# Four in place of six seven-product pairs in the fourth group of the convolution's input

## The chip, the cores and the metric

The kernel runs on one core of a Trainium2 chip. The metric is device time in microseconds (us) from start to end of one execution; the time of a kernel is the median of its runs. Engines are named as the profile names them: PE (TensorE, matmuls), PEld (its weight loads), DVE (VectorE), ACT (ScalarE), POOL (GpSimd), SP (the queue that issues the loads).

## The reference, cut to what matters

One layer with two halves side by side, 256 rows of 4096 columns. Seven column blocks of one large weight `w_in` are multiplied with the normalised input; the convolution half needs the blocks `a_c` and `g_c`.

```python
xn = rms_norm(h, norm_in_g[i])
proj = xn @ w_in[i]                       # 256x4096 @ 4096x14336
q, k, v, z_a, a_c, g_c, z_c = jnp.split(proj, ...)
y_a = rms_norm(chunked_attention(q, k, v, rel_table[i]), attn_out_g[i]) * silu(z_a)
y_c = rms_norm(conv_module(a_c, g_c, ...), conv_out_g[i]) * silu(z_c)
h = h + concatenate([y_a, y_c]) @ w_out[i]
h = h + sigmoid(rms_norm(h) @ w_ple_gate[i] + b) * (p[i] @ w_ple[i])
# conv_module: u = a * sigmoid(g); causal depthwise convolution of 31 taps;
# layer norm; silu; u @ w_pw + b_pw
```

## The kernel before

All large products have 256 rows and 4096 (or 2048) rows of weights. `mixed_product` makes one such product for two column blocks of 512 at once (a *group*). It walks the 4096 weight rows as sixteen *pairs* of 128-row blocks in the order of a list such as `early`. Every float32 operand is split in a high and a low part (`wh`, `wl` of weights, `uh`, `ul` of sums of weights), and each product is three matmuls of 128x128 by 128x512: high by high, low by high, high by low (line 372).

- A pair without a star is *plain*: 2 row halves x 2 column blocks x 2 weight blocks = 8 products, 24 matmuls. Its two weight tiles are each split by one ACT cast and one DVE subtraction of 128x1024 (lines 204 and 205).
- A starred pair (*seven*) is done by a scheme of Strassen's kind with 7 products, 21 matmuls. For that, DVE forms four sums of weights (`ua`, `ub`, lines 428, 429, 432, 433), ACT and DVE split the two sum tiles (again lines 204 and 205), and four combinations of the pair's x are needed.
- The combinations of x for one pair are six DVE instructions (line 280, then 257 to 260, and 266) and one ACT cast (265). For pairs 0, 2, 4 and 6 they are made in the first group and kept for all later ones.

The groups run in this order: convolution input 1 (`glu_conv(0)`, ends near 103 us of the span), 2 (to 191 us), queries and keys, values, attention 0, convolution input 3, convolution input 4 (454 to 546 us), queries and keys 1, attention 1, and so on to attention 3 near 930 us, where the pointwise convolution (`w_pw`) starts. At the end of each convolution group DVE finishes the four results `z` (496), multiplies by the gate (707), PE transposes (714) and ACT copies to `uT` (719).

The convolution itself is elementwise DVE work, 124 instructions for each group (the *taps*, lines 678 and 682). Taps and other small jobs wait in the list `later`; `fill(n)` takes n of them at the end of each pair, by `early_fills` (64 in all for a group). Behind the taps stand the jobs of the layer norm: sums, mean, variance (775), spread (788), `swish` (DVE 793, ACT 794) and `split` (ACT 804, DVE 805). The program is written in that order, and a scheduler of the framework then sets the order on each engine; every engine works its own list strictly in that order.

In `glu_conv(3)` (the fourth group) the list is `early_six`: pairs 8 and 10 have stars too, and `more_combinations` makes the x combinations for them inside the group, ahead of pairs 7 and 9, as four jobs at the head of `later`.

Of the kernel before, what the change touches and what calls it, by code (L numbers as in the profile page):

```python
# [11 lines left out]
F32R = mybir.dt.float32r  # L12
# [4 lines left out]
P = 128  # L17
NB = 512
# [7 lines left out]
def hybrid_block(  # L26
# [24 lines left out]
    _, T, D = x.shape  # L51
    NH = T // P
    AW = attn_out_g.shape[1]
    CW = conv_out_g.shape[1]
# [13 lines left out]
    def pool(name, bufs, stack=ctx, side=0, **kw):  # L68
        return stack.enter_context(tc.tile_pool(name=name, bufs=bufs, side=sides[side], **kw))

    cpool = pool("cpool", 1)
    act = pool("act", 8)
# [13 lines left out]
    def tmp_psum():  # L86
        return ps_tmp.tile([P, 512], F32, tag="tmp", name="tmp_ps")
# [7 lines left out]
    o_a, o_g, o_zc = 4 * AW, 4 * AW + CW, 4 * AW + 2 * CW  # L95
    w_in0 = w_in[0]
# [83 lines left out]
    later = deque()  # L180
# [95 lines left out]
    def combine_again(dst, at, t, i, rows, then=lambda ins: None):  # L276

        a, s = rows
        then(
            nc.vector.tensor_tensor(  # L280
                a.rearrange("q (i t) -> q i t", t=T), t[:, i : i + 2, 0, :].bitcast(F32),
                t[:, i : i + 2, 1, :].bitcast(F32), ALU.add,
            )
        )
        return combined_parts(dst, at, s, a[:, :T], a[:, T : T + P], a[:, T + P :], 1.0, then)
# [27 lines left out]
    def units(text):  # L313

        return [(int(u.rstrip("*")), u.endswith("*")) for u in text.split()]
# [2 lines left out]
    dense = units("1 0* 3 2* 5 4* 6* 7 8* 9 10* 11 12* 14* 13 15")  # L318
    first = units("0 1 3 5 7 9 11 13 15 2* 8 4* 10 6* 12 14")
    early = units("1 3 5 7 0* 9 2* 11 4* 13 6* 15 8 10 12 14")  # L320
    early_six = units("1 3 5 7 0* 9 2* 11 4* 13 6* 15 8* 10* 12 14")

    valued = units("1 3 5 7 8 0* 9 2* 10 4* 11 6* 12 13 14 15")

    early_fills = (4, 6, 7, 1, 5, 1, 5, 1, 5, 1, 2, 4, 6, 6, 6, 4)
# [155 lines left out]
    def scaled_pair(w, col, apart, order, r, fills, home={}, then=lambda: None, **kw):  # L481

        t, z = [], []

        def on_helpers(helper):
            for dst, src in zip((t, z), sum_tiles(**home)):
                dst.extend(src)
            then()
            nc.scalar.activation(z[0][0], helper["P1"], AF.Identity, scale=r[:, :1])
            helper_sums(helper, z)  # L490
            for h, j in QUARTERS[1:]:
                nc.scalar.activation(z[h][j], z[h][j], AF.Identity, scale=r[:, h : h + 1])

        c = mixed_product(w, col, xT, xS, order, on_helpers, fills=fills, apart=apart, **kw)
        for h, j in QUARTERS:
            stt(
                z[h][j], c[h][j], r[:, h : h + 1], z[h][j],
                ALU.mult, ALU.subtract if j else ALU.add,
            )
        return t  # L500
# [16 lines left out]
    xS = {}  # L517
# [6 lines left out]
    r_x = cpool.tile([P, NH], F32, name="r_x")  # L524

    def combinations(c, then=lambda ins: None):

        rest = []

        def begin():  # L530
            rows = spool.tile([P, 2, NB], F32, tag="stage", name="comb")
            rest.append(
                combine_again(*xS[2 * c], xT[c], 0, (rows[:, 0], rows[:, 1]), then)
            )

        return begin, lambda: rest.pop()()
# [147 lines left out]
                cv[:, i, PAD - k :], ALU.mult, ALU.add,  # L684
            )

    def more_combinations(pair):

        if pair in (7, 9):
            c = (pair + 1) // 2  # L690
            xS[2 * c] = act.tile([P, 2, 2, T], F32R, tag="act", name="comb_x"), 0
            later.extendleft(reversed(combinations(c)))

    def glu_conv(c):
        if c == 0:
            sg, gate = scaled_pair(
                w_in0, o_a, o_g - o_a, first, r_x, (1,), begin=first_pairs
            )
        else:
            last = c == CW // NB - 1  # L700
            sg, gate = scaled_pair(
                w_in0, o_a + c * NB, o_g - o_a, early_six if last else early, r_x, early_fills,
                ahead=more_combinations if last else None,
            )
        for h in range(NH):
            nc.scalar.activation(gate[:, h, :], gate[:, h, :], AF.Sigmoid)
            tt(sg[:, h, :], sg[:, h, :], gate[:, h, :], ALU.mult)
        uT = spool.tile([P, 4, T], F32, tag="hd", name="uT", bufs=5)
        for pair in range(2):
            pt = tmp_psum()  # L710
            for i in range(2):
                for h in range(NH):
                    b = 2 * pair + i
                    nc.tensor.transpose(
                        pt[:, i * T + h * P : i * T + (h + 1) * P],
                        sg[:, h, b * P : (b + 1) * P],
                        ident,
                    )
            nc.scalar.copy(
                uT[:, 2 * pair : 2 * pair + 2, :], pt.rearrange("q (i t) -> q i t", t=T)  # L720
            )
        cv = act.tile([P, 4, T], F32, tag="act", name="cv")
        for i in range(4):
            for k in reversed(range(TAPS)):
                later.append(partial(conv_tap, cv, uT, i, 4 * c + i, k))
        conv.append(cv)
# [201 lines left out]
    n_g = H // GH  # L928
    assert n_g == CW // NB == 4
    glu_conv(0)  # L930
    glu_conv(1)
    load_bias(0)
    keys(0, early_fills)
    values(0, early, early_fills, home=dict(tag="hd", bufs=5))
    attention(0)
    glu_conv(2)
    glu_conv(3)
    load_bias(1)
# [69 lines left out]
    xS = [xS[0][0]]  # L1008
# [22 lines left out]
    def before_last(make):  # L1031

        return lambda pair: make(0) if pair == dense[-1][0] else None
# [20 lines left out]
    for ys, o_z, r_y in ((y_a, o_za, r_a), (y_c, o_zc, r_c)):  # L1054
        for c0 in range(0, len(ys), 2):
            last = ys is y_c and c0 + 2 == len(ys)
# [27 lines left out]
    for c0 in range(0, D // NB, 2):  # L1084
        for j in range(2):
            hc = act.tile([P, NH, NB], F32, tag="act", name="hc")
            c = c0 + j
# [5 lines left out]
        def on_helpers(helper):  # L1093
# [10 lines left out]
            ahead=y_ahead if c0 == 0 else before_last(h_ahead) if c0 + 2 == D // NB else None,  # L1104
# [205 lines left out]
```

## Time and profile before

| | |
|---|---|
| median of 3 runs | 2048.03 us (2047.39 to 2050.57) |
| the profiled execution | 2048.88 us, its span 2047.1 us |
| PE busy | 2022.0 us (99%), 9082 matmuls recorded |
| PEld busy | 1656.1 us (81%) |
| DVE busy | 1943.8 us (95%) |
| ACT busy | 1195.2 us (58%) |
| mean granted clock of PE | 0.996 |

The busy time of PE counts overlapping matmuls once, so idle time of PE is read from gaps ahead of single matmuls, and slow stretches from the granted clock. A row of the timeline gives start, length, engine, line, what is written and read, and in square brackets how long the engine idled just before and what ended that. A row of the chain of waits gives a start, a length and the instruction that the end of the stretch was waiting for at that time.

### The profile page before, as it was taken

The page shows a single profiled execution, that of the slowest core. Times are in us where ns is not written, and L with a number is a line of the kernel's source. Part 1 is how long each engine was busy: PE and PEld are TensorE (multiplying, and loading weights), DVE is VectorE, ACT ScalarE, POOL GpSimd, SP SyncE. Part 2 cuts the span into 40 slices and gives each one's busy share as a digit, 9 for nine tenths or more (in the row PEclk, how much of TensorE's full clock was granted, in tenths as well). Part 3 has the DMA queues.
Part 4 walks back from the last instruction along what each step waited for, and adds up shares of the span by engine and source line. Part 5 has one row for each costly group of instructions (what it writes and reads, how often), then busy time and mean ns, then how long its engine had stood idle before and what let it go on. Part 6 is the DMA issues. An engine that isn't in the chain of part 4 may idle for free.

```text
span 2047.1 us, 26034 instructions
## 1 busy us (share of the span) xinstructions
PE 2022.0 (99%) x9082; PEld 1656.1 (81%) x9082; DVE 1943.8 (95%) x2784; ACT 1195.2 (58%) x1543; POOL 8.1 (0%) x19
## 2 busy tenths in 40 slices
PE   9999999999999999999999999999999999999997
PEld 7888888888778888878888888888888888888876
DVE  7999999989999999889899999999999999999998
ACT  7655545655555544676565656676565666655555
POOL 0000000000000000000000000000000000000000
PEclk9999999999999999999999999999999999999998
DMA  8666666566665666645666666676666656666765
GB/s 288 192 197 205 204 192 200 165 203 185 192 187 170 199 198 183 191 155 199 192 213 210 193 214 200 216 242 208 214 198 206 204 188 208 199 220 205 235 207 179
DMA packets 157758, 412.30 MB, mean 201 GB/s; under 512 B 12974, under 2 KB 16190, under 8 KB 157626
## 3 DMA queue, kind: packets, MB, share of 16 engines
q1 hardware_dynamic: 156976, 409.80, 63.5%
q8 instruction: 71, 1.16, 0.2%
q10 hardware_dynamic: 650, 0.84, 0.1%
q14 instruction: 61, 0.50, 0.1%
HBM read 406.39 MB, written 4.19 MB: 201 GB/s over the span
## 4 chain that ended last, share of the span: by engine, by line
PE 88%; DVE 7%; issue 2%; DMA 1%; ACT 1%; SPq 0%; POOL 0%; POOLq 0%; ACTq 0%; DVEq 0%
PE acc L372 69%; PE acc_P L372 16%; DVE wl L205 2%; DVE cv L682 2%; PE tmp_ps L170 1%; DVE ul L205 1%; PE acc L218 1%; DMA wt<-in_w_in_dram 1%; DVE ub L433 0%; PE tmp_ps L835 0%; PE tmp_ps L851 0%; DVE ub L432 0%; DMA wt<-in_w_out_dram 0%; ACT wh L204 0%; PE tmp_ps L869 0%
## 5 line engine op out<-in xcount | busy, mean ns | idle before, releaser
L372 PE MATMUL acc<-wh,big_t 128*128 128x512 f32 x4196 | 1296.9, 392 | 2.5 <-ACT wh L204 1.0
L204 ACT CAST wh<-wt 128x1024 fp32r<-128x1024 f32 (+1 forms) x737 | 711.1, 976 | 561.0 <-PE acc L372 416.2
L372 PEld LDWEIGHTS acc<-wh,big_t 128*128 128x128 f32 x4196 | 784.9, 188 | 166.3 <-ACT wh L204 1.8
L205 DVE TENSOR_TENSOR wl<-wt,wh 128x1024 fp32r<-128x1024 f32 (+1 forms) x737 | 819.5, 1123 | 36.6 <-ACT wh L204 32.4
L372 PE MATMUL acc<-wl,big_t 128*128 128x512 f32 x2098 | 805.6, 392 | 2.8 <-DVE wl L205 2.7
L372 PEld LDWEIGHTS acc<-wl,big_t 128*128 128x128 f32 x2098 | 393.4, 188 | 87.8 <-DVE wl L205 6.1
L682 DVE SCALAR_TENSOR_TENSOR cv<-uT,dw,cv 128x255 f32<-128x255 f32 (+22 forms) x480 | 212.1, 460 | 1.0
L204 ACT CAST uh<-ub 128x1024 fp32r<-128x1024 f32 x130 | 136.7, 1052 | 114.0 <-DVE ub L433 97.4
L204 ACT CAST uh<-ua 128x1024 fp32r<-128x1024 f32 x130 | 136.9, 1053 | 82.2 <-DVE ua L429 76.5
L205 DVE TENSOR_TENSOR ul<-ub,uh 128x1024 fp32r<-128x1024 f32 x130 | 158.4, 1219 | 7.0 <-ACT uh L204 6.3
L372 PE MATMUL acc_P<-uh,big_t 128*128 128x512 f32 x528 | 161.6, 393 | 0.0
L205 DVE TENSOR_TENSOR ul<-ua,uh 128x1024 fp32r<-128x1024 f32 x130 | 158.3, 1218 | 0.8 <-ACT uh L204 0.2
L372 PEld LDWEIGHTS acc_P<-uh,big_t 128*128 128x128 f32 x528 | 97.4, 188 | 24.3 <-ACT uh L204 5.1
L428 DVE TENSOR_TENSOR ua<-wt 128x512 f32<-128x512 f32 x130 | 89.0, 685 | 18.1 <-DMA wt<-in_w_in_dram 11.4
L372 PE MATMUL acc_P<-ul,big_t 128*128 128x512 f32 x264 | 101.1, 394 | 1.2 <-DVE ul L205 1.2
L429 DVE TENSOR_TENSOR ua<-wt 128x512 f32<-128x512 f32 x130 | 88.7, 683 | 1.8 <-DMA wt<-in_w_in_dram 1.1
L433 DVE TENSOR_TENSOR ub<-ub,wt 128x512 f32<-128x512 f32 x130 | 88.9, 684 | 0.9
L432 DVE TENSOR_TENSOR ub<-ua,wt 128x512 f32<-128x512 f32 x130 | 88.7, 683 | 0.3
L372 PE MATMUL acc<-uh,big_t 128*128 128x512 f32 x260 | 80.6, 390 | 0.0
L372 PE MATMUL acc_P<-wh,big_t 128*128 128x512 f32 x260 | 80.4, 389 | 0.0
L372 PE MATMUL acc_P<-uh,comb_t 128*128 128x512 f32 x228 | 69.8, 391 | 0.1
L372 PEld LDWEIGHTS acc_P<-ul,big_t 128*128 128x128 f32 x264 | 49.2, 188 | 15.2 <-DVE ul L205 5.0
(240 smaller groups left out, 1370.1 us busy)
## 6 DMA issues: line engine op xcount, KB each, us to landing
wt<-in_w_in_dram SPq DMA_DIRECT2D x447, 512.0 KB, 4.2
wt<-in_w_out_dram SPq DMA_DIRECT2D x128, 512.0 KB, 4.1
wt<-in_w_ple_gate_dram SPq DMA_DIRECT2D x128, 512.0 KB, 4.2
wt<-in_w_pw_dram SPq DMA_DIRECT2D x32, 512.0 KB, 4.5
hc<-in_x_dram SPq DMA_DIRECT2D x8, 512.0 KB, 5.8
wt<-in_w_ple_dram SPq DMA_DIRECT2D x8, 512.0 KB, 4.5
xin<-in_x_dram SPq DMA_DIRECT2D x7, 512.0 KB, 7.9
out_dram<-hc SPq DMA_DIRECT2D x12, 256.0 KB, 2.8
```

The lines of the kernel that those rows point to most:

```text
L170: nc.tensor.transpose(pt[:, i * T + h * P : i * T + (h + 1) * P], src[:, h, b] if len(src.shape) == 4 else src[:, h, b * P : (b + 1) * P], ...
L204: nc.scalar.copy(wh[:, :kc, :], wt[:, :kc, :]),
L205: nc.vector.tensor_tensor(wl[:, :kc, :], wt[:, :kc, :], wh[:, :kc, :].bitcast(F32), ALU.subtract),
L218: nc.tensor.matmul(acc, a, b[:, k, :], start=kb == 0 and kind == 0, stop=kb == kblocks - 1 and kind == 2,)
L372: nc.tensor.matmul(banks[name], a, b, start=name not in begun, stop=final and ends[name] == n and kind == 2 and not (left and name in "P2 ...
L428: plus(ua[:, 0], w0[:, 0], w0[:, 1])
L429: plus(ua[:, 1], w0[:, 1], w1[:, 1])
L432: plus(ub[:, 0], ua[:, 0], w1[:, 1])
L433: plus(ub[:, 1], ub[:, 0], w1[:, 0])
L682: nc.vector.scalar_tensor_tensor(cv[:, i, PAD - k :], uT[:, i, : T + k - PAD], dw[:, b, k : k + 1], cv[:, i, PAD - k :], ALU.mult, ALU.add,)
```

## The change

The fourth group uses the list `early`, as the second and third groups do: pairs 8 and 10 become plain. `more_combinations` and its four jobs at the head of `later` are gone, and with them the two tiles `comb_x`. Nothing else is edited. Lines behind the first removed one move up by one, and those behind `more_combinations` by nine: in the rows below 371 is the old 372, 677 and 681 are 678 and 682, 785 is 794.

```diff
     early = units("1 3 5 7 0* 9 2* 11 4* 13 6* 15 8 10 12 14")
-    early_six = units("1 3 5 7 0* 9 2* 11 4* 13 6* 15 8* 10* 12 14")
...
-    def more_combinations(pair):
-
-        if pair in (7, 9):
-            c = (pair + 1) // 2
-            xS[2 * c] = act.tile([P, 2, 2, T], F32R, tag="act", name="comb_x"), 0
-            later.extendleft(reversed(combinations(c)))
-
...
-            last = c == CW // NB - 1
             sg, gate = scaled_pair(
-                w_in0, o_a + c * NB, o_g - o_a, early_six if last else early, r_x, early_fills,
-                ahead=more_combinations if last else None,
+                w_in0, o_a + c * NB, o_g - o_a, early, r_x, early_fills,
+                
             )
```

Since each fill takes as many jobs as before, all later jobs come four places earlier, and the scheduler sets a different order from the fourth group (454 us) up to the pointwise convolution (about 1000 us). Three places matter below.

DVE at the start of the fourth group, behind the gate's products (`comb` is a combination of x, `cv` a tap). Before:

```order
L280 TENSOR_TENSOR comb<-big_t 128x512
L678 TENSOR_SCALAR cv<-uT,dw,prm 128x256
L257 TENSOR_TENSOR comb<-comb 128x128
L682 SCALAR_TENSOR_TENSOR cv<-uT,dw,cv 128x255
L258 SCALAR_TENSOR_TENSOR comb<-comb 128x128
L682 SCALAR_TENSOR_TENSOR cv<-uT,dw,cv 128x254
L205 TENSOR_TENSOR wl<-wt,wh 128x1024
```

The same place with the change:

```order
L677 TENSOR_SCALAR cv<-uT,dw,prm 128x256 x2
L681 SCALAR_TENSOR_TENSOR cv<-uT,dw,cv 128x255 x2
L681 SCALAR_TENSOR_TENSOR cv<-uT,dw,cv 128x254
L205 TENSOR_TENSOR wl<-wt,wh 128x1024
L681 SCALAR_TENSOR_TENSOR cv<-uT,dw,cv 128x253
L681 SCALAR_TENSOR_TENSOR cv<-uT,dw,cv 128x254
```

Taps have taken the places of the combinations. From the last `z` of the third group to the last `z` of the fourth, DVE's list had 147 instructions, 57 of them taps; it now has 138, 72 of them taps. That is, in kind and number, the list of the second group (138, 72 taps), and nearly in its order. PE has 375 instructions between the last transposes of the third and fourth groups before and 381 now; the second group has 386.

ACT behind the spread of the layer norm (`rs`), near 882 us, up to the second weight cast (`wh`) that follows it. Before:

```order
L743 ACTIVATE rs<-tmp_ps 128x256
L204 CAST wh<-wt 128x1024
L794 ACT_TABLE_LOAD
L794 ACTIVATE cv<-cv,prm 128x256 x3
L492 ACTIVATE z<-z,r_x 128x512
L794 ACTIVATE cv<-cv,prm 128x256 x2
L492 ACTIVATE z<-z,r_x 128x512 x2
L794 ACTIVATE cv<-cv,prm 128x256 x6
L204 CAST wh<-wt 128x1024
L794 ACTIVATE cv<-cv,prm 128x256 x4
```

With the change:

```order
L734 ACTIVATE rs<-tmp_ps 128x256
L204 CAST wh<-wt 128x1024
L785 ACT_TABLE_LOAD
L785 ACTIVATE cv<-cv,prm 128x256 x7
L491 ACTIVATE z<-z,r_x 128x512 x3
L785 ACTIVATE cv<-cv,prm 128x256 x8
L204 CAST wh<-wt 128x1024
L785 ACTIVATE cv<-cv,prm 128x256
```

Fifteen swishes in place of eleven now stand ahead of the second cast. On PE the first matmul that reads this cast is the 45th behind the spread's transposes before, and the 49th now.

PE at the first head of attention 3, near 909 us (`kT,qT` the scores, `ident,s` the transposes of the softmax, `acc_80..` the first pair of the pointwise convolution). Before:

```order
L851 MATMUL tmp_ps<-kT,qT 128x256
L372 MATMUL acc_8092<-wh,big_t 128x512
L372 MATMUL acc_8094<-wh,big_t 128x512 x2
L869 MATMUL tmp_ps<-ident,s 128x128 x3
L372 MATMUL acc_8091<-wl,big_t 128x512
L372 MATMUL acc_8093<-wl,big_t 128x512
```

With the change:

```order
L842 MATMUL tmp_ps<-kT,qT 128x256
L371 MATMUL acc_8052<-wh,big_t 128x512
L371 MATMUL acc_8052<-wl,big_t 128x512
L371 MATMUL acc_8054<-wh,big_t 128x512 x2
L371 MATMUL acc_8054<-wl,big_t 128x512
L371 MATMUL acc_8051<-wh,big_t 128x512 x2
L371 MATMUL acc_8053<-wh,big_t 128x512 x2
L371 MATMUL acc_8052<-wh,big_t 128x512 x2
L371 MATMUL acc_8054<-wh,big_t 128x512 x2
L371 MATMUL acc_8051<-wl,big_t 128x512
L371 MATMUL acc_8053<-wl,big_t 128x512
L371 MATMUL acc_8052<-wl,big_t 128x512
```

One more matmul follows and then the first transpose: 17 matmuls stand between the scores and it, where 3 stood. DVE's split of the first pointwise weights (`wl`) has also moved ahead of the last four `z`, where it stood behind the softmax's row maxima.

## The prediction

> **What bounds the kernel now.** I read the page first, then busy time by stretch, the chain of waits inside the fourth group, and the timeline of PE for its gaps.
>
> ```profile
> PE 2022.0 (99%) x9082; PEld 1656.1 (81%) x9082; DVE 1943.8 (95%) x2784; ACT 1195.2 (58%) x1543; POOL 8.1 (0%) x19
> PE 88%; DVE 7%; issue 2%; DMA 1%; ACT 1%; SPq 0%; POOL 0%; POOLq 0%; ACTq 0%; DVEq 0%
> ```
>
> PE bounds the whole, with DVE close behind. So the question is which of them bounds the one group that is edited. Busy time by stretch, from one group's first `uT` copy to the next one's, for the second group (four sevens) and the fourth (six); the columns are length, then busy time and count on PE, PEld, DVE, ACT, POOL, then granted clock:
>
> ```profile
> 103.70:191.20 87.50, 87.45 (x388) 71.11 (x387) 87.09 (x139) 44.66 (x50) 0.00 (x0) 1.00 0.64 193
> 454.10:546.20 92.10, 88.56 (x378) 69.74 (x376) 91.83 (x149) 49.06 (x55) 0.24 (x1) 0.98 0.62 183
> ```
>
> The fourth group has fewer matmuls and takes 4.6 us longer. PE idles 3.54 us in it (92.10 - 88.56), against 0.05 in the second; DVE never rests. The chain of waits between 518 and 527 us says which work PE waits for, and the timeline of PE shows the gaps (square brackets):
>
> ```profile
> by line: DVE cv L682 30.9%; DVE ul L205 25.2%; issue 16.1%; DVE ub L433 8.3%; DVE wl L205 7.5%; DVE ub L432 6.7%; DVE ua L428 6.7%; DVE ua L429 6.7%
> ...
> 519.51 1.13 DVE ul L205
> 520.65 0.39 DVE cv L682
> 521.03 0.60 DVE ua L428
> 521.63 0.39 DVE cv L682
> 522.02 0.60 DVE ua L429
> ```
> ```profile
> 523.81 1.56 PE L372 MATMUL acc_P<-uh,comb_x 128*128 128x512 f32 x4 [2.37 <-ACT uh L204]
> ```
> ```profile
> 536.51 1.20 PE L372 MATMUL acc<-wl,big_t 128*128 128x512 f32 x4 [0.50 <-DVE wl L205]
> ...
> 547.09 1.20 PE L372 MATMUL acc<-wl,big_t 128*128 128x512 f32 x4 [0.63 <-DVE wl L205]
> ```
>
> The whole chain is DVE working down its list. The 2.37 us wait names ACT, but that cast had itself waited for `ua` on DVE, with taps ahead of it. After 2.37 us of idling the clock drops too. The same windows show the rule by which it drops here:
>
> ```profile
> 1596.00:1599.40 3.40, 2.18 (x10) 1.51 (x9) 3.40 (x4) 0.77 (x2) 0.00 (x0) 1.00 0.44 131
> 910.15:913.56 3.41, 1.56 (x7) 0.71 (x6) 3.41 (x10) 1.24 (x5) 0.00 (x0) 1.00 0.01 2
> 521.03:524.44 3.41, 1.04 (x5) 0.55 (x4) 3.41 (x7) 1.68 (x3) 0.00 (x0) 1.00 0.23 38
> 524.45:527.85 3.40, 3.40 (x10) 2.66 (x9) 3.40 (x7) 1.26 (x2) 0.00 (x0) 0.50 0.36 135
> 913.57:916.97 3.40, 3.40 (x13) 3.03 (x13) 3.26 (x6) 1.30 (x4) 0.00 (x0) 0.50 0.57 170
> ```
>
> Behind the two stretches of 3.41 us in which PE idled 2.37 and 1.85 us, PE ran 3.4 us at half clock, which costs 1.7 us each time. Behind the one with 1.22 us idle it did not. So the price of a stall jumps by 1.7 us somewhere between 1.22 and 1.85 us of idling.
>
> The Trainium skill, "TensorE: Matmul & The Clock Gate", Part 1, has a window of 3413 ns, which agrees with these stretches. It also says that the clock falls after at least one idle window of about 3.4 us, and that gaps beyond about 3.4 us are to be avoided; here 1.85 us were enough, and the trace decides. By the page neither stall would have cost clock.
>
> **The change part by part.** *Matmuls.* Two pairs go from 21 to 24 matmuls. A stretch of the chain with nothing but matmuls gives the step:
>
> ```profile
> 475.91 6.12 PE acc L372 x27
> ```
>
> 6.12 / 27 = 0.2267 us, so 6 x 0.2267 = +1.36 us on PE. Nothing can hide that when PE is the bound.
>
> *DVE work in the group.* Rows of the fourth group and of all combinations (count | busy, mean ns):
>
> ```profile
> L280 DVE TENSOR_TENSOR comb<-big_t 128x512 f32<-128x512 f32 x2 | 1.4, 680 | 0.0
> ...
> L266 DVE TENSOR_TENSOR comb_x<-comb,comb_x 128x512 fp32r<-128x512 f32 x2 | 1.4, 676 | 0.0
> ```
> ```profile
> L257 DVE TENSOR_TENSOR comb<-comb x30: 274/284/293, 28.9 to 1716.1; 128x128 f32<-128x128 f32 x30
> ```
>
> By the steps of the chain above, a seven's four sums are 4 x 0.60 and its two splits 2 x 1.13; one weight split grows from half width (0.60, as a sum of that width) to 1.13. That is 4.1 us a pair, 8.3 for two. A combination is 0.68 + 4 x 0.28 + 0.68 = 2.5 us by durations and about 2.0 by steps: 4 to 5 for two. Against that stand 15 more taps that the new list pulls into the group, 15 x 0.39 = 5.9. Net -6.4 to -7.4 us of DVE, so 84.4 to 85.4 us of its 91.8 are left. The rows of the second group, whose list is the same in kind and number, say 87.1 as the upper end. PE's need, from that group too: 87.5 less 5 x 0.2267, since the fourth now has 381 instructions where that has 386, is 86.4. I take 86.4: PE sets the end again, and the group goes from 92.1 to 86.4, **-5.7 us**. If DVE needs its 87.1 to 87.5 it is -4.6 to -5.0. The added matmuls are in this figure. From below: idle 3.54, half clock 1.7 and about 1.9 of short waits are 7.1, less 1.36. ACT loses 4 casts of sums and 2 of combinations and is half idle: no effect.
>
> *The start of the next group.* The 0.63 us wait at 547.09 is the same lateness of DVE, with a slow first matmul behind it: **-0.8 us**, at least nothing, since the second group has no such gap.
>
> *Taps and layer norm four places earlier.* No weight transfer moves, but the order changes up to 1000 us. Most of it is covered: PE idles 0.18 us in 80 here.
>
> ```profile
> 700.00:780.00 80.00, 79.82 (x356) 64.63 (x355) 79.33 (x127) 37.86 (x41) 0.31 (x1) 1.00 0.67 200
> ```
>
> In such places the new order can gain 0.6 us (short waits that go) or lose about 1.5 (three new waits of 0.5, like the one at 536.51). I take **+0.4**. Three places are larger.
>
> ```profile
> 881.48 0.68 PE L788 MATMUL tmp_ps<-lnsum,mean_w 128*128 128x128 f32 x4 [0.42 <-DVE lnsum L787]
> ```
>
> The spread's transposes stood 4 matmuls behind the variance, and 144 stand between them now: **-0.5 us**, with the slow matmul behind the gap.
>
> ```profile
> 889.15 3.05 ACT L794 ACTIVATE cv<-cv,prm 128x256 f32<-128x256 f32 x6
> 892.11 1.03 ACT L204 CAST wh<-wt 128x1024 fp32r<-128x1024 f32 x1
> 893.04 2.08 ACT L794 ACTIVATE cv<-cv,prm 128x256 f32<-128x256 f32 x4
> ```
> ```profile
> 893.19 1.66 PE L372 MATMUL acc<-wh,big_t 128*128 128x512 f32 x6 [1.01 <-ACT wh L204]
> ```
>
> PE waits 1.01 us for a weight cast behind eleven swishes. Four more (2.08 us) now stand ahead of that cast, and 4 more matmuls (0.9) cover: the wait grows to 2.2, or +1.2; 0.1 comes back at the next cast, which has less ahead of it. So +1.1. An idle time of 2.2 us is above the 1.85 that cost clock, if most of it falls in one stretch of 3.41. I take it that it does: +1.7, together **+2.8 us**, with +1.1 as the other end.
>
> ```profile
> 909.38 0.60 PE L851 MATMUL tmp_ps<-kT,qT 128*128 128x256 f32 x2
> ...
> 911.42 0.33 PE L869 MATMUL tmp_ps<-ident,s 128*128 128x128 f32 x1 [0.75 <-ACT s L862]
> 911.91 0.44 PE L869 MATMUL tmp_ps<-ident,s 128*128 128x128 f32 x2 [0.16 <-ACT s L862]
> 913.28 1.85 PE L372 MATMUL acc<-wl,big_t 128*128 128x512 f32 x4 [0.93 <-DVE wl L205]
> ```
>
> The softmax takes 911.42 - 909.38 = 2.0 us from scores to transposes, with 3 matmuls (0.7) over it; 17 now cover 3.9. The weight split for which PE then waits has moved ahead of the softmax. So 0.75 + 0.16 + 0.93 = 1.84 us of idling go, and the half clock behind (1.7): **-3.4 us** with a remainder of 0.1, between 0 and -3.5.
>
> The sum: -5.7 - 0.8 + 0.4 - 0.5 + 2.8 - 3.4 = **-7.2 us**. All of it lies inside the span, so the profiled execution would go from 2047.1 to 2039.9 of span, 2048.88 to 2041.7 with the 1.78 us around it. It was 0.85 above the median; for the median I forecast 2048.03 - 7.2 = **2040.8 us**.
>
> **The rivals.** *The gaps stay (slower).* DVE's list in the group fills up with taps, 15 more, and each stands between two steps of a weight sum, as in the chain above; if those taps keep the sums as late as now, PE still waits 7.1 us and pays 1.36 on top: 2048.03 + 1.36 = 2049.4. It speaks for it that taps are the largest share of the chain; against it that the second group runs the same list with 0.05 us of PE idle. It decides if more than 5.7 of the 7.1 us stay.
>
> *Given back at the pointwise convolution.* The longer run of swishes costs 2.8, and DVE is late at the softmax anyway, so that its 3.4 stays: -5.7 - 0.8 + 0.4 - 0.5 + 2.8 = -3.8, 2044.2 us. For it: the chain there runs through DVE as well as ACT, and the same layer-norm jobs are still queued. Against: the split that PE waited for stands earlier.
>
> *No half clock at all.* The swish stall stays under the jump, or is split between two stretches: 1.7 less, and without the allowance of 0.4: 2040.8 - 2.1 = 2038.7. For it: the jump is only bracketed. By what the Trainium skill, "TensorE: Matmul & The Clock Gate", Part 1, says of gaps, no stall of 2.2 us would trip the clock.
>
> **How the numbers follow.** The forecast has 0.42, with its own range 2039.4 to 2042.4. The rival without half clock has 0.26, the one that gives back 0.23, the slower one 0.05; 0.04 is left for something unnamed. The range 2037.6 to 2045.2 leaves out the slower rival, the unnamed and a little of the ends: low, the 2038.7 with the short waits' 0.6 and some more; high, the 2044.2 with 1.0 if DVE needs its 87.1 us. A measurement of this kernel can tell about 0.2%, 4.1 us, from no change: below 2043.9 is faster. The forecast and the rival without half clock are, and of the one that gives back a little under half (0.10); so faster 0.78, within 0.2% 0.19, slower 0.03.
>
> **What would show it.** Right: the fourth group takes about 86.4 us from `uT` copy to `uT` copy, PE idles under 0.3 us in it, and no half clock at 524; the stall on the cast behind the swishes is near 2.2 us with half clock behind it; the transposes of attention 3's first head wait for nothing. Wrong: PE gaps behind `ua` or `ub` in the fourth group as before, or new gaps of over 1 us between 550 and 880 us, which I priced at 0.4 in all.

## The result, and the profile after

Seven runs each: 2041.94 us median with the change (2039.13 to 2043.05) against 2047.39 before (2045.95 to 2050.66). The ratio is 0.9968, its 95% interval 0.9958 to 0.9978: faster by 0.2 to 0.4%. The profiled execution took 2041.64 us, 1.74 of it outside its span.

The head of the page, and the line with the engines:

```profile
span 2039.9 us, 26023 instructions
...
PE 2018.6 (99%) x9088; PEld 1657.7 (81%) x9088; DVE 1929.4 (95%) x2760; ACT 1190.0 (58%) x1537; POOL 8.5 (0%) x19
```

The span fell by 7.2 us. DVE lost 14.4 us of busy time in the whole kernel (1943.8 before), twice that; only 5.7 us of them lie in the fourth group's row (91.83 before, 86.11 below). Busy time by stretch, as shown of before: the second group, the fourth, two stretches at the swishes, the softmax of attention 3, and 700 to 780 us.

```profile
103.24:190.74 87.50, 87.37 (x386) 70.88 (x385) 86.88 (x139) 44.66 (x49) 0.00 (x0) 1.00 0.63 193
454.11:541.10 86.99, 86.16 (x385) 70.48 (x383) 86.11 (x138) 44.64 (x49) 0.00 (x0) 1.00 0.63 190
884.26:887.67 3.41, 1.49 (x6) 1.24 (x7) 1.51 (x3) 3.41 (x8) 0.00 (x0) 1.00 0.30 115
887.67:891.08 3.41, 3.41 (x10) 2.66 (x9) 3.28 (x6) 3.41 (x7) 0.00 (x0) 0.50 0.48 168
903.00:911.00 8.00, 8.00 (x38) 6.15 (x37) 7.24 (x16) 4.78 (x8) 0.00 (x0) 1.00 0.25 84
...
700.00:780.00 80.00, 79.06 (x355) 64.81 (x354) 79.85 (x124) 38.03 (x41) 0.31 (x1) 1.00 0.64 195
```

The fourth group now looks like the second: PE idles 0.83 us in it (86.99 - 86.16; 3.54 before) and keeps its clock, and DVE has some 0.9 us to spare where it had 0.3. The softmax costs PE nothing. The swishes cost more than before: 1.92 us idle in one stretch of 3.41 us (3.41 - 1.49), and the next one at half clock. The rows of PE with idle time of 0.3 us or more ahead of them, from 454 to 960 us, are these six and no others:

```profile
484.06 0.50 PE L371 MATMUL acc_P<-ul,comb_t 128*128 128x512 f32 x1 [0.83 <-DVE ul L205]
...
715.38 0.33 PE L826 MATMUL tmp_ps<-ident,z 128*128 128x128 f32 x1 [0.50 <-DVE z L495]
716.04 2.19 PE L826 MATMUL tmp_ps<-ident,z 128*128 128x128 f32 x15 [0.33 <-DVE z L495]
...
886.18 1.68 PE L371 MATMUL acc<-wh,big_t 128*128 128x512 f32 x6 [2.63 <-ACT wh L204]
...
953.04 0.70 PE L371 MATMUL acc<-wh,big_t 128*128 128x512 f32 x2 [0.34 <-DVE y_c L990]
954.75 0.73 PE L371 MATMUL acc<-wh,big_t 128*128 128x512 f32 x2 [0.32 <-DVE y_c L990]
```

The page's chain of waits can't be set beside that of before. It reaches back only to 886 us, where PE waits for the cast behind the swishes, so its shares add up to 56% of the span (PE 52%, DVE 2%); before it covered nearly all of it (PE 88%, DVE 7%).

To see where the 7.2 us came from, the *lost time* of PE is added up by stretch: for each matmul, the distance from its start to the next one's start, less the median distance of its kind (0.227 us for 128x512). Idle time, slow first matmuls and half clock are all in it. Two executions of each kernel were profiled; the second ones are the runs `before_again` and `after_again` further down.

| stretch of the program | before | after | before, again | after, again | forecast of the change |
|---|---|---|---|---|---|
| up to the fourth group | 3.78 | 3.82 | 3.48 | 3.73 | 0 |
| fourth group | 8.72 | 1.41 | 8.75 | 0.87 | -7.1 |
| to the scores of attention 1 | 1.72 | 0.07 | 1.75 | 0.07 | -0.8 |
| to the spread, with the wait ahead of it | 6.48 | 4.82 | 6.26 | 5.71 | -0.1 |
| spread and swishes | 1.60 | 4.95 | 1.62 | 3.33 | +2.8 |
| scores of attention 3 and behind | 5.40 | 1.67 | 3.78 | 1.67 | -3.4 |
| the rest | 6.11 | 8.40 | 5.36 | 6.14 | 0 |
| six matmuls more | | +1.36 | | +1.36 | +1.36 |
| span | 2047.1 | 2039.9 | 2044.3 | 2036.2 | -7.2 |

The columns add up to -7.3 and -8.1, the spans to -7.2 and -8.1. The same program differs from itself by 2.8 and 3.7 us of span from one execution to the next.

### The profile page after: what moved, and what is told of

It reads as the page before. It is cut to its first block, busy times and chain, and to the rows that moved or that the text cites. A ratio compares the mean times of both kernels' runs of the same rounds, so it can differ in the third digit from the quotient of the medians.

```text
span 2039.9 us, 26023 instructions
## 1 busy us (share of the span) xinstructions
PE 2018.6 (99%) x9088; PEld 1657.7 (81%) x9088; DVE 1929.4 (95%) x2760; ACT 1190.0 (58%) x1537; POOL 8.5 (0%) x19
## 4 chain that ended last, share of the span: by engine, by line
PE 52%; DVE 2%; issue 1%; DMA 1%; ACT 0%; POOLq 0%; POOL 0%; ACTq 0%; DVEq 0%
PE acc L371 38%; PE acc_P L371 12%; PE acc L218 1%; DVE wl L205 1%; PE tmp_ps L170 1%; DMA wt<-in_w_in_dram 0%; DVE ul L205 0%; PE acc L359 0%; DMA wt<-in_w_out_dram 0%; ACT wh L204 0%; DVE ub L431 0%; DVE hc L1100 0%; DVE ua L428 0%; PE tmp_ps L860 0%; PE tmp_ps L842 0%
## 5 line engine op out<-in xcount | busy, mean ns | idle before, releaser
L371 PE MATMUL acc<-wl,big_t 128*128 128x512 f32 x2112 | 814.7, 391 | 0.0
L681 DVE SCALAR_TENSOR_TENSOR cv<-uT,dw,cv 128x249 f32<-128x249 f32 (+22 forms) x480 | 207.6, 460 | 0.6
L204 ACT CAST uh<-ua 128x1024 fp32r<-128x1024 f32 x128 | 134.8, 1053 | 85.4 <-DVE ua L428 80.1
```

The lines of the kernel that those rows point to most:

```text
L204: nc.scalar.copy(wh[:, :kc, :], wt[:, :kc, :]),
L371: nc.tensor.matmul(banks[name], a, b, start=name not in begun, stop=final and ends[name] == n and kind == 2 and not (left and name in "P2 ...
L681: nc.vector.scalar_tensor_tensor(cv[:, i, PAD - k :], uT[:, i, : T + k - PAD], dw[:, b, k : k + 1], cv[:, i, PAD - k :], ALU.mult, ALU.add,)
```

## The experiments

Two theories of the fourth group. The first: it ends when DVE is through its list, so what counts is the length of that list against PE's 86.2 us. The rival: the chain of a seven (sums on DVE, cast on ACT, split on DVE) makes the gaps wherever two more sevens stand, whatever else DVE does. A second question is what the new order of the later jobs, four places earlier, did behind the group. The run of the kernel before in each comparison is on the same chip.

| run | what differs | median us | before, us | ratio, 95% |
|---|---|---|---|---|
| four_empty | the change, four empty jobs | 2039.39 | 2047.51 | 0.9958, 0.9945 to 0.9970 |
| four_combos | the change, combinations still made | 2042.48 | 2047.51 | 0.9973, 0.9962 to 0.9983 |
| five | five sevens | 2042.57 | 2047.51 | 0.9974, 0.9964 to 0.9985 |
| three | three sevens | 2041.11 | 2047.51 | 0.9968, 0.9956 to 0.9981 |
| six_moved | six sevens, 18 jobs fewer in the group | 2046.87 | 2048.05 | 0.9991, 0.9982 to 1.0000 |
| swish_early | the change, earlier layer norm | 2034.90 | 2048.05 | 0.9938, 0.9926 to 0.9951 |
| six_swish | before, earlier layer norm | 2046.76 | 2048.80 | 0.9991, 0.9982 to 1.0000 |
| empty_swish | four_empty, earlier layer norm | 2038.30 | 2048.80 | 0.9946, 0.9933 to 0.9960 |

**Four empty jobs in place of the combinations.** All jobs behind them keep the places that they had before; only the group's own work changes.

```diff
+        if pair in (7, 9):
+            later.extendleft([lambda: None] * 2)
```

> The changed kernel with four empty jobs at the two places where the jobs of the combinations were taken in, so that all later jobs keep the places that they had before. This parts the fourth group from what the earlier places did near 880 to 915 us. Theory 1 (the vector list of the fourth group was too long for PE): the group takes 87 us from uT copy to uT copy as with the change, and the end looks as before: PE idles about 1.0 us at the weight cast behind eleven swishes with no half clock there, and about 1.8 us at attention 3's first head with half clock behind it; against the changed kernel -3.4 and +3.7 there and +0.6 at the spread, so about 1 us more than it, ratio to before 0.9973. Rival (most of the gain came from the later order): the group may still be quick, but the kernel is within 2 us of before, ratio above 0.999.

The fourth group, and the stretch of 3.41 us with PE's waits at the softmax of attention 3, with the one behind it:

```profile
454.29:540.86 86.57, 86.27 (x385) 70.47 (x383) 86.24 (x139) 44.45 (x49) 0.00 (x0) 1.00 0.63 191
903.18:906.59 3.41, 2.31 (x12) 1.62 (x13) 3.41 (x9) 1.47 (x3) 0.00 (x0) 1.00 0.14 37
906.59:910.00 3.41, 3.41 (x19) 2.89 (x19) 3.41 (x8) 1.82 (x6) 0.00 (x0) 1.00 0.72 235
```

The group gains as much as with the change. At the end the places are as before: the wait behind the swishes is 1.02 us again, the softmax's waits of 0.74 and 0.94 us are back. But no half clock follows, since only 1.10 us of these (3.41 - 2.31) fell in one stretch. So the group alone is worth the whole gain; what the four places moved, gains and losses together, is worth nothing that these intervals can tell, and if anything it cost a little (0.9958 against 0.9968). The half clock that I expected at the softmax, and with it 1 us more than with the change, did not come.

> Four sevens with empty jobs, profiled once more. Its first profile had the 1.84 us stall at attention 3's first head without half clock. By stretches that run on by themselves, half clock may follow this time, and the span is then 1.7 us longer (2039.3 in place of 2037.6); by the stall alone there is none again and the span is within 0.5 us.

A second profile of the same kernel had a span of 2036.6 us, the same waits (1.01 in one stretch, 1.10 in the other) and again no half clock.

**Combinations made and not read.** Four sevens as with the change, but DVE and ACT still make the combinations for pairs 8 and 10, which nothing reads.

```diff
+        if pair in (7, 9):
+            c = (pair + 1) // 2
+            xS[2 * c] = act.tile(..., name="comb_x"), 0
+            later.extendleft(reversed(combinations(c)))
```

> Four sevens as in the changed kernel, but the two combinations of x are still made in the group (nobody reads them). Only the two sevens are gone. Theory 1 (length of the vector list): the list is 4 to 5 us longer, of which taps that move out give some back; between the group's last z and the next group's it would take 89 to 90 us, the PE waits 2 to 3 us more than with the change, ratio to before 0.9985. Rival (the sevens' chain, sum then cast then split, with taps between, was what PE waited for, and the combinations were cover): the group takes 87 us all the same, ratio 0.997 as with empty jobs.

```profile
454.30:542.33 88.03, 87.31 (x384) 70.00 (x382) 87.67 (x146) 45.85 (x51) 0.31 (x1) 1.00 0.63 192
904.87:908.28 3.41, 1.79 (x7) 1.11 (x8) 3.41 (x10) 1.96 (x5) 0.00 (x0) 1.00 0.03 6
908.28:911.69 3.41, 3.41 (x13) 3.07 (x13) 3.11 (x7) 1.18 (x4) 0.00 (x0) 0.50 0.69 227
```

DVE is busy 1.4 us longer than in four_empty (87.67 against 86.24) and the group lasts 1.5 us longer (88.03 against 86.57): the combinations cost what they take from DVE. That is the smaller part: with the combinations still made the group is already 4.1 us shorter than before (92.10 - 88.03), by the two sevens' sums and splits. The wait at the softmax has the same length as in four_empty, falls with 1.62 us in one stretch, and half clock follows. I had expected more of the combinations, 89 to 90 us for the group and a ratio of 0.9985; the group also has four taps fewer than in four_empty (69 against 73), which gives part of DVE's time back.

**Five and three sevens.** In the first, against the kernel before, one pair of the two is made plain and its combinations are left out; in the second, against the change, pair 6 of the fourth group loses its star too. Only the lines that matter:

```diff
-    early_six = units("1 3 5 7 0* 9 2* 11 4* 13 6* 15 8* 10* 12 14")
+    early_six = units("1 3 5 7 0* 9 2* 11 4* 13 6* 15 8* 10 12 14")   # five
-        if pair in (7, 9):
+        if pair == 7:                                                 # five
+    early_three = units("1 3 5 7 0* 9 2* 11 4* 13 6 15 8 10 12 14")   # three, fourth group alone
```

> Five sevens: pair 8 starred, pair 10 plain, one combination. PE needs 85.7 us in the group. Theory 1: the vector list lies between, 88 to 89 us for the group, so half to two thirds of the 5.2 us are won there; the end keeps the old shape (twelve swishes ahead of the cast, 4 matmuls between scores and transposes): ratio to before 0.998. Rival (a threshold: any sixth or fifth seven is one too many once DVE is full): the group takes 90 us or more, ratio 0.999 to 1.0.

```profile
454.96:541.98 87.02, 86.10 (x381) 69.72 (x379) 87.02 (x140) 46.77 (x52) 0.31 (x1) 1.00 0.63 194
```

> Three sevens: pair 6 is plain as well. PE needs 87.0 us in the group. Theory 1 (with four, PE is the bound again): another 0.68 us of matmuls and next to nothing to win, since PE idles under 1 us there; the group takes 87.2 us, and the order at the end is that of the changed kernel: 0 to 0.7 us slower than the changed kernel, ratio to before 0.9968 to 0.9972. Rival (DVE is still the bound with four, its list reads 87 us too): the group and the next get faster by 1 us or more, ratio below 0.9963.

```profile
453.75:539.68 85.93, 85.57 (x383) 70.28 (x381) 85.67 (x142) 43.21 (x47) 0.00 (x0) 1.00 0.64 192
```

With five, DVE has no idle time in the group (87.02 of 87.02) and PE loses 2.6 us there; with four PE loses 0.9 to 1.4, with three 0.8, while PE's own work grows by 0.68 a step. (The two ends of such a row are copies whose place among the matmuls shifts by a few, so the lengths of rows with different lists are good to about 1.4 us, six matmuls; the lost time is not touched by this.) The first of the two pairs bought most of the gain, more than the 88 to 89 us that I expected; the second bought the rest, and a third buys nothing. In the totals five, four and three can't be told apart, since other places behind the group differ too: five waits 2.00 us behind the swishes and 2.19 at the softmax, with half clock behind the latter, and three 2.64 behind the swishes, with half clock for 6.8 us.

**Six sevens with room on DVE.** The group keeps its six sevens and their combinations, but its fills take 46 jobs in place of 64; a later group takes 82 in all.

```diff
     early_fills = (4, 6, 7, 1, 5, 1, 5, 1, 5, 1, 2, 4, 6, 6, 6, 4)
+    light_fills = (4, 4, 5, 1, 3, 1, 3, 1, 3, 1, 1, 3, 4, 4, 4, 4)   # fourth group
-    blocks((o_q + 3 * NB, o_v + 2 * NB), early, (4,))
+    blocks((o_q + 3 * NB, o_v + 2 * NB), early, (5, 5, 5, 5, 5, 5, 5, 6, ...))
```

> Six sevens and both combinations as before, but the fourth group takes 46 jobs from the list in place of 64, and the group of the fourth queries and third values (which has the shortest vector list) 82 in place of 64; all later jobs keep their places, and the order from the layer norm on is that of before. Theory 1 (what PE waited for was the length of the vector list, whoever fills it): the list goes from 105.0 to 98.1 us by durations, about as with five sevens (99.2) or with idle combinations (100.3), so the lost time of the group falls from 8.7 to 2 to 3 us, and as PE needs 1.36 us less than with four the group takes 86 to 87 us; ratio to before 0.9965 to 0.9975. Rival (the sevens' own chain of sum, cast and split is too long for the order in which they stand): the group stays above 90 us, ratio above 0.999.

```profile
453.76:541.31 87.55, 86.89 (x384) 70.40 (x383) 87.55 (x134) 49.58 (x57) 0.00 (x0) 1.00 0.64 192
...
772.78:776.19 3.41, 1.68 (x7) 1.09 (x7) 3.41 (x6) 2.93 (x4) 0.00 (x0) 1.00 0.19 28
776.19:779.60 3.41, 3.41 (x10) 2.63 (x9) 3.41 (x5) 2.12 (x3) 0.00 (x0) 0.50 0.53 160
```

The rival falls: with all its sevens the group loses 2.1 us in place of 8.7, and the wait of 2.4 us and its half clock are gone. It is DVE's length that counts. The durations of all DVE instructions that start between the two copies add up to 97.6 us here and to 97.6 us in five as well (103.2 before): with the same length, six sevens lose 2.1 us and five lose 2.6. But the total moved by 0.1% only, where I had expected 0.25% or more, since the taps that left came due elsewhere: between the scores of attention 1 and 2 the lost time rose from 3.2 to 8.05 us, with these waits and the half clock above behind the second:

```profile
752.00 0.50 PE L373 MATMUL acc_P<-ul,comb_t 128*128 128x512 f32 x1 [1.14 <-DVE ul L205]
...
775.49 0.73 PE L373 MATMUL acc<-wl,big_t 128*128 128x512 f32 x2 [1.73 <-DVE wl L205]
```

So the change gains because there is less work for DVE, not because the work stands elsewhere: the one other group that was tried had no room for it.

**The layer norm earlier.** If the wait behind the swishes comes from where they stand, taking more jobs out of `later` at the start of the last group ahead of attention 3 must remove it. The sum of the fills stays the same in the first of the three runs; the other two take three jobs more.

```diff
-    valued, (5, 5, 4, 5, 4, 2, 3, 2, 3, 2, 3, 4, 4, 4, 4, 4)
+    valued, (6, 6, 5, 6, 5, 2, 3, 2, 3, 2, 3, 3, 3, 3, 3, 3)   # swish_early
+    valued, (7, 7, 6, 6, 5, 2, 3, 2, 3, 2, 3, 3, 3, 3, 3, 3)   # six_swish, empty_swish
```

> The changed kernel, where the group ahead of the pointwise convolution takes 6, 6, 5, 6, 5 jobs in its first five pairs (5, 5, 4, 5, 4 before) and 3 in place of 4 in its last five. The spread then comes some pairs earlier, and weight casts stand between the swishes, never more than three swishes in a row; scores and transposes of attention 3's first head stay 15 apart. Theory (the stall at the weight cast is the run of swishes ahead of it): the 2.6 us and the half clock go, lost time between spread and scores falls from 5.0 to about 1, ratio to before 0.9945 to 0.9955. Rival (the work is only moved: DVE and ACT are then late in the pairs into which the swishes went): new waits of 2 us or more ahead of 880 us, ratio 0.996 to 0.997.

```profile
454.36:541.01 86.65, 86.17 (x385) 70.48 (x383) 86.10 (x138) 44.66 (x50) 0.00 (x0) 1.00 0.63 191
835.00:890.00 55.00, 55.00 (x248) 45.65 (x247) 52.56 (x81) 43.87 (x67) 1.61 (x1) 1.00 0.64 199
880.00:930.00 50.00, 50.00 (x246) 41.31 (x245) 41.94 (x81) 31.70 (x60) 1.06 (x1) 1.00 0.54 179
```

> The kernel before, six sevens and all, with only the fills of the group ahead of the pointwise convolution changed (7, 7, 6, 6, 5 in the first five pairs, 3 in the last five), so that casts stand between the swishes and 15 matmuls between scores and transposes. This takes the end's part out of the comparison. If the two places are independent, the fourth group still loses 8.7 us and the end gains what it gained on four sevens: spread wait 0.4, swish stall 1.0, softmax 1.84 and at times half clock: 4 to 6 us, ratio to before 0.997 to 0.998. Rival (DVE has no time for the earlier layer norm with six sevens): new waits of DVE between 800 and 880 us take 2 us or more of it, ratio 0.9985 or above.

```profile
841.74:845.15 3.41, 0.88 (x5) 0.68 (x5) 3.41 (x4) 1.76 (x2) 0.00 (x0) 1.00 0.51 156
845.15:848.56 3.41, 3.41 (x10) 2.63 (x9) 3.41 (x5) 0.35 (x1) 0.30 (x1) 0.50 0.88 273
...
880.00:930.00 50.00, 50.00 (x243) 41.54 (x242) 45.02 (x85) 35.49 (x66) 0.00 (x0) 1.00 0.54 174
```

> Four sevens, empty jobs in place of the combinations' jobs, and the earlier layer norm: the parts that gained, together. Against the changed kernel with earlier layer norm alone the later jobs stand four places later, and the waits for z before the transposes near 716 us (0.7, 0.3, 0.1) should be gone as in the first kernel with empty jobs: 0.5 to 1.5 us faster than that, ratio to before 0.993 to 0.9938. Rival (those waits are of no weight, and what they cover comes back elsewhere): the same within 0.5 us.

```profile
835.39:838.80 3.41, 1.19 (x5) 1.01 (x6) 3.41 (x5) 2.11 (x2) 0.31 (x1) 1.00 0.56 162
838.81:842.22 3.41, 3.41 (x9) 2.63 (x9) 3.41 (x5) 0.00 (x0) 0.00 (x0) 0.50 0.91 290
```

In swish_early PE idles nowhere from 835 to 930 us and keeps its clock all the way; at 2034.90 us it is the fastest version, somewhat better than expected (0.9938 where I had 0.9945 to 0.9955). Its span is 7.2 us shorter than that of the change (2032.7 against 2039.9), and 5.0 of them lie at the spread and the swishes, where the lost time fell from 4.95 us to nothing. In the other two the wait behind the swishes went as well, but a new one of 2.5 us came at the spread, with half clock. The timeline of DVE in six_swish shows why:

```profile
834.30 1.22 DVE L205 TENSOR_TENSOR ul<-ua,uh 128x1024 fp32r<-128x1024 f32 x1
835.43 4.78 DVE L760 TENSOR_TENSOR cv<-cv,mu 128x256 f32<-128x256 f32 x14
840.13 1.22 DVE L768 TENSOR_TENSOR sq<-sq 128x1024 f32<-128x1024 f32 x1
841.27 0.41 DVE L760 TENSOR_TENSOR cv<-cv,mu 128x256 f32<-128x256 f32 x1
841.60 1.22 DVE L768 TENSOR_TENSOR sq<-sq 128x1024 f32<-128x1024 f32 x1
842.74 0.42 DVE L760 TENSOR_TENSOR cv<-cv,mu 128x256 f32<-128x256 f32 x1
843.07 2.35 DVE L205 TENSOR_TENSOR wl<-wt,wh 128x1024 fp32r<-128x1024 f32 x2
```

All sixteen centerings (subtractions of the mean) and two squares stand in one run of 7.6 us (835.43 to 843.07), ahead of the weight split for which PE waits. In empty_swish the same run lasts from 828.70 to 836.34 us. In swish_early, whose later jobs stand four places earlier, PE forms the mean at 803 us (826 in empty_swish, 832 in six_swish), and the centerings come in six runs of at most four, spread from 807 to 829 us. So the gain of swish_early rests on the new order as well as on the fills, and the room on DVE alone was not enough: empty_swish has that too. The expectation of empty_swish, 0.5 to 1.5 us faster than swish_early, is a miss; without that wait it would have been about 4 us faster (an estimate: 2.5 us idle and 1.7 of half clock). On the kernel before, the earlier layer norm is worth next to nothing (0.9991), which is what the rival of its expectation said. The fills of swish_early were not tried on the kernel before.

**The same kernels once more.** No edit; a second profile of each.

> The kernel before, profiled once more. If the half clock depends on where a stall falls in stretches of 3.41 us that run on by themselves, the same stalls of 2.4 us at 521 us and 1.84 us at 910 us appear at the same places of the program, but half clock follows them only in some executions: more surely behind the longer one. If it depends on the stall alone, both are followed by half clock again.

> The changed kernel, profiled once more. The stall at the weight cast behind fifteen swishes is 2.6 us again. If half clock comes only when most of a stall falls in one stretch of 3.41 us, a stall of 2.6 us leaves more than 1.3 us in one in any case, and mostly more than 1.85: I expect half clock again, and a span within 1 us of 2039.9; without it 1.7 us less.

Before, again: the stretch with the wait at the softmax, and the one behind it.

```profile
908.95:912.36 3.41, 1.92 (x9) 0.97 (x7) 3.01 (x8) 0.98 (x4) 0.00 (x0) 1.00 0.01 2
912.36:915.77 3.41, 3.06 (x17) 2.63 (x18) 3.41 (x9) 2.19 (x4) 0.00 (x0) 1.00 0.47 148
```

After, again: the fourth group, and the three stretches at the swishes.

```profile
454.01:540.47 86.46, 86.13 (x385) 70.49 (x383) 86.12 (x138) 44.66 (x49) 0.00 (x0) 1.00 0.63 191
881.41:884.83 3.42, 2.36 (x10) 1.30 (x8) 1.48 (x3) 3.42 (x8) 0.00 (x0) 1.00 0.31 64
884.83:888.24 3.41, 1.79 (x8) 1.49 (x9) 1.81 (x3) 3.41 (x8) 0.00 (x0) 1.00 0.23 90
888.24:891.65 3.41, 3.41 (x17) 2.78 (x16) 3.28 (x6) 3.41 (x7) 0.00 (x0) 1.00 0.59 190
```

The wait behind the swishes was 2.65 us again, yet, against the expectation, no half clock followed: 1.06 us of idling fell in one stretch, 1.62 in the next. And of the kernel before, the waits of 0.75 and 0.94 us at the softmax had no half clock behind them this time (1.49 us idle in one stretch), as the first profile had.

## Why the prediction held, step by step

The total: -7.2 us of span as forecast in the first pair of profiles, -8.1 in the second; the medians of the comparison differ by 5.45 us (2047.39 - 2041.94), where 7.2 was forecast; 2041.94 stands beside 2040.8. The terms were less good than their sum: they miss by up to 2.3 us, the misses cancel, and the same program differs by 2.8 and 3.7 us from one execution to the next. That the first pair gave 7.2 to the tenth is luck.

- *The fourth group* (-5.7): -7.31 + 1.36 = -5.95 of lost time in the first pair, -7.88 + 1.36 = -6.5 in the second; between the `uT` copies 92.16 went to 86.99 and 92.20 to 86.46. Right in size and in cause, by four_combos, five and six_moved. PE's idle time was to be under 0.3 us; 0.83 and 0.33 were measured. In the first, PE waits 0.83 us at 484 us for the split of a sum: DVE is still close to full. The prediction's own sum left DVE 84.4 to 85.4 us in the group; it was busy 86.11, nearer to the second group's 87.1, which the prediction had as the upper end.
- *The next group's start* (-0.8): -1.65 and -1.68. The 0.63 us at 547 went, and a wait of 0.33 at 601 us with it, which I had not counted.
- *The order up to the spread* (+0.4, and -0.5 for the wait ahead of the spread): -1.7 and -0.6. The spread's wait of 0.42 us went. New waits at the transposes of 715 us (0.50 and 0.33) stand against some that went.
- *The swishes* (+2.8): +3.35 and +1.71. The wait grew from 1.01 to 2.63 us, not to 2.2, so that the idle part is +1.6 in place of +1.1. The step that failed is the start of ACT's run, as the rows below show. The other part, 1.7 us of half clock, was there in the first profile and not in the second. The prediction took it that most of the wait falls in one stretch; whether it does changes from one execution to the next.
- *The softmax* (-3.4): -3.73 and -2.11. The waits went in both, as forecast. The half clock that they took with them was there in one profile of the kernel before and not in the other.
- *The rest* (0): +2.3 and +0.8. Two waits for `y_c` at the end of a pointwise group are new (0.34 and 0.32, some 1.0 us with the slow matmuls behind them); I had not followed DVE so far. Most of what is left lies around and beyond 1000 us, where both kernels run the same list, and changes between executions of one kernel.

The rows of ACT behind the spread, before and after:

```profile
882.20 0.39 ACT L743 ACTIVATE rs<-tmp_ps 128x256 f32<-128x256 f32 x1 [1.88 <-PE tmp_ps L788]
882.48 1.04 ACT L204 CAST wh<-wt 128x1024 fp32r<-128x1024 f32 x1
...
892.11 1.03 ACT L204 CAST wh<-wt 128x1024 fp32r<-128x1024 f32 x1
```
```profile
872.37 0.39 ACT L734 ACTIVATE rs<-tmp_ps 128x256 f32<-128x256 f32 x1
873.49 1.05 ACT L204 CAST wh<-wt 128x1024 fp32r<-128x1024 f32 x1 [0.72 <-PE acc L371]
...
875.86 3.56 ACT L785 ACTIVATE cv<-cv,prm 128x256 f32<-128x256 f32 x7
879.33 1.94 ACT L491 ACTIVATE z<-z,r_x 128x512 f32<-128x512 f32 x3
881.17 4.03 ACT L785 ACTIVATE cv<-cv,prm 128x256 f32<-128x256 f32 x8
885.11 1.03 ACT L204 CAST wh<-wt 128x1024 fp32r<-128x1024 f32 x1
```

The spread now comes earlier against PE's matmuls, so the first cast behind it waits 0.72 us until PE has done with a buffer (before, that cast followed the spread at once), and all swishes stand behind that cast. From `rs` to the second cast ACT takes 12.74 us (885.11 - 872.37), 9.91 before (892.11 - 882.20): 2.83 more, of which I had counted the 2.08 of four swishes and left out this wait.

The two half clocks were therefore not one term of +1.7 and one of -1.7 but two draws of which each profile shows one outcome. Of the rivals, the gaps that stay and the gain that is given back are excluded by the group's rows and the softmax's. The rival without half clock describes the second profile: it has none up to the end of PE's work, and its 2038.03 us stand beside the 2038.7 of that rival.

Of the other runs only the mean granted clock is known, to three digits. In the thirteen profiles of this case it is 0.998 where no stretch between the start and the end of PE's work ran at half clock, 0.997 where one did and 0.996 where two did. Of the seven runs of the change five have 0.997 (2041.64 to 2043.05 us, the median among them) and two have 0.998 (2039.13 and 2040.08). So the median seems to stand for the case with one half clock, as the forecast had it. The profile of before, from which the forecast started, had two; of the 44 runs of that kernel that stand beside the experiments 15 have 0.996, 22 have 0.997 and 7 have 0.998. If its median has one, the change in half clock drops out, and 7.2 less 1.7 is 5.5, close to the 5.45 measured. The start and the end of a run weigh in this rounded figure too, so this is an indication and not shown.

## What to carry to other kernels

A scheme that saves matmuls by adding elementwise work pays until the helper engine is as long as the matmuls in that stretch; find the crossing by busy time of both engines per stretch (here 86.1 of DVE against 86.2 of PE with four sevens, 87.0 against 86.1 with five), not over the whole kernel. Taking work off the helper beats moving it when the stretch that would take it is full as well. After such a change the steps behind it are worth another look: moving a few jobs of the layer norm earlier brought another 0.3% on top of the change. Look at the order that results and not only at the number of jobs: nearly the same move on the other order put all centerings in one run and brought little.

## What was not expected of the hardware

Half clock depends not on the length of a wait but on how much of it falls in one stretch of a grid of 3.41 us that runs on by itself. Its onsets in one execution lie whole stretches apart: with a stretch of 3.4133 us, the onsets before at 524.45, 913.57 and 2036.55 us are 114.0 and 329.0 stretches apart, and those in six_moved at 776.19 and 912.72 us are 40.0. Sorted by PE's idle time within such a stretch, over all profiles: 1.66, 1.73, 1.84, 1.92, 2.0, 2.2, 2.3, 2.4 and 2.5 us were each followed by 3.4 us at half clock; 0.9 to 1.2, 1.4 and 1.5 never; at 1.62 us four_combos was, after_again was not. In three, 1.97 us idle in one stretch and 0.7 in the next were followed by two stretches at half clock. So a wait of 2.65 us can pass and one of 1.84 us cost 1.7 us more, by its place in the grid.

The Trainium skill, "TensorE: Matmul & The Clock Gate", Part 1, asks for at least one idle window of about 3.4 us for the clock to fall. These runs agree with the window's length and not with the rule: about half of a window idle was enough.
